# Other prices for VectorE, ScalarE and TensorE in a planner that interleaves side streams with matmuls, and a wait for free memory places in one stream

## The chip, the cores and the metric

The kernel runs on one core of a Trainium2 chip. Five engines work side by side, each through its own instructions in order: TensorE (PE in the profile: matmuls, and PEld: its weight loads), VectorE (DVE), ScalarE (ACT), GpSimd (POOL) and SyncE (SP), which here starts transfers. Semaphores make an engine wait for another. The metric is the device time of one execution in microseconds (us).

## The reference

One layer with a prompt of 512 tokens and 8 samples of 16 tokens each, 640 tokens in all, in float32. Every token goes through a wide input product, whose columns feed three branches; their gated sum goes through a normed residual and a feed-forward part.

```python
z = x @ w_in
xa, ya, glu, q, gates = jnp.split(z, COL_SPLITS, axis=-1)
xa_c = causal_depthwise_conv(xa_hist, conv_a_w, conv_a_b)
h, h_last = rg_lru(xa_c, h_prev, lru_w_r, lru_b_r, lru_w_i, lru_b_i, lru_lambda)
out_a = (h * jax.nn.gelu(ya)) @ proj_a
u = glu[..., :D_CONV] * jax.nn.sigmoid(glu[..., D_CONV:])
v = causal_depthwise_conv(u_hist, conv_b_w, conv_b_b)          # 31 taps, 512 channels
out_b = jax.nn.silu(layer_norm(v, ln_b_g, ln_b_b)) @ proj_b
out_c = mem_cross_attention(q, mem_k, mem_v) @ proj_c          # 4 heads, 256 memory rows
merged = g[:, :, 0] * out_a + g[:, :, 1] * out_b + g[:, :, 2] * out_c
x = layer_norm(DEEPNORM_ALPHA * x + merged @ w_out, ln1_g, ln1_b)
ffn = (jax.nn.silu(x @ w_ffn_gate) * (x @ w_ffn_up)) @ w_ffn_down
x = layer_norm(DEEPNORM_ALPHA * x + ffn, ln2_g, ln2_b)
```

## The kernel before

Data lie with features on the 128 partitions and the 640 tokens along the free side. A float32 product is made of three products of a shorter type (xh by wh, xl by wh, xh by wl, where h is the rounded part and l the rest), so each weight tile is copied (wh, on ScalarE) and its rest subtracted (wl, on VectorE, or on POOL for every second step from 12 to 35: line 305).

The program is a list of 304 steps. A step of w_in makes 128 output columns: 8 blocks of the inner size, times three products, times two halves of 320 tokens, 48 matmuls into two accumulators named pu, and then an evacuation that reads them. There are four pu accumulators, so step i+2 can start only when step i has been evacuated. Steps 8 to 11 and 16 to 19 make the glu columns, 12 to 15 the queries, 20 to 27 xa, 28 to 35 gates, 36 to 43 are proj_c's, which need the attention's output.

Beside the steps run side streams, written as generators: `b` (the convolution of 31 taps over four tiles k = 0 to 3, all on VectorE, its states and its norm ln_b), `attn` (the prompt's attention in four row tiles t, then the samples'), `lru` and `a`. Their small matmuls go to two other accumulators named pv; `room()` lets a stream go on when one is free. Each engine's program order is fixed when the program is written, by a planner: every issued instruction adds its price (`price_vector`, `price_scalar`, `price_tensor`) to a clock of its engine, and between two half steps `advance()` lets the streams issue work as long as the clocks of VectorE and ScalarE are behind that of TensorE:

```python
while max(V.time, 0 if name in vector_next else A.time) < P.time:
    c = next(gen)
```

`finish(name)` issues all that is left of a stream at once. A stream holds its temporary tiles in 52 memory places; `slots_left(n)` yields while fewer than n are free.

Four places matter. `softmax_start` reads a score accumulator with a maximum on VectorE (mx), its negative (nm), and four exponentials on ScalarE; it is called for each t of the prompt and for the samples. `conv_b_taps(k)` issues 30 pairs of VectorE instructions for tile k, of 128x(512 minus the tap) and 128x128. `conv_b_states` stands between tiles 1 and 2. ln_b begins with a sum of the four tiles on POOL (lines 853 and 855), which a matmul by the tile `ones` reads. Nearly all engine instructions are recorded on line 64, where the planner's wrapper calls the engine.

Of the kernel before, what the change touches and what calls it, by code (L numbers as in the profile page):

```python
# [39 lines left out]
def view(x, shape):  # L40

    n = 1
    for d in shape[1:]:
        n *= d
    x = x[:shape[0], :n]
    if len(shape) == 3:
        x = x.rearrange("p (a b) -> p a b", a=shape[1])
    elif len(shape) == 4:
        x = x.rearrange("p (a b c) -> p a b c", a=shape[1], b=shape[2])
    return x  # L50
# [17 lines left out]
def elements(x):  # L68
    n = 1
    for d in x.shape[1:]:  # L70
        n *= d
    return n


def price_vector(e, name, a, k):
    if name in ("tensor_reduce", "bn_stats"):
        return 70 + elements(a[1]) / 0.96
    n = elements(a[0])
    if name == "tensor_tensor_scan":
        return 70 + 2 * n / 0.96  # L80
    if name in ("tensor_scalar", "tensor_copy", "memset"):
        return 70 + n / 1.92
    return (130 if name == "scalar_tensor_tensor" else 70) + n / 0.96


TABLES = {AF.Exp: "e", AF.Tanh: "esgl", AF.Sigmoid: "s", AF.Sqrt: "q", AF.Silu: "l", AF.Gelu_apprx_tanh: "g"}
# [2 lines left out]
def price_scalar(e, name, a, k):  # L89
    if name != "activation":  # L90
        return 100
    t = 130 + elements(a[0]) / 1.2
    t += 93 * sum(1 for z in ("scale", "bias", "accum_out") if z in k and not isinstance(k[z], float))
    need = TABLES.get(a[2])
    if need is not None and (e.table is None or e.table not in need):
        e.table = need[0]
        t += 1283
    return t


def price_tensor(e, name, a, k):
    n = elements(a[0])
    if a[1].dtype == F32R:
        return n / 2.4 + 2.5
    if a[0].shape[0] == 32:
        return n / 2.4
    return max(105.0, (n if name == "transpose" else 4 * n) / 2.4)


class Slots:  # L110
# [7 lines left out]
    def get(self, shape, dtype=F32):  # L118
        if not self.free_list:
            raise RuntimeError("no slot is free")  # L120
        i = self.free_list.pop(0)
        self.low = min(self.low, len(self.free_list))
        self.count += 1
        x = self.pool.tile([128, T], dtype, name=f"s{i}_{self.count}", tag=f"s{i}", bufs=1)
        x = view(x, shape)
        self.at[id(x)] = (i, x)
        return x

    def free(self, *xs):
        for x in xs:  # L130
            i, _ = self.at.pop(id(x))
            self.free_list.append(i)
# [11 lines left out]
def trunk(ctx, tc, x_prompt, x_sample, mem_prompt, state_conv_a, state_lru, state_conv_b, cache_mem_k, cache_mem_v,  # L144
# [4 lines left out]
          new_conv_a_s, new_lru_s, new_conv_b_s):  # L149
    nc = tc.nc  # L150
    V, A, P = Engine(nc.vector, price_vector), Engine(nc.scalar, price_scalar), Engine(nc.tensor, price_tensor)
    G, S = nc.gpsimd, nc.sync

# [15 lines left out]
    def slots_left(n):  # L169
        while len(slots.free_list) < n:  # L170
            yield None
# [7 lines left out]
    def pv():  # L179
        assert side[0] < 2  # L180
        side[0] += 1
        return ps.tile([128, 2, 512], F32, name="pv", tag="v", bufs=2)

    def room(n=1):
        while side[0] + n > 2:
            yield None

    def over(n=1):
        side[0] -= n
# [16 lines left out]
    def split(hi, lo, src, eng=V):  # L206
        copy(hi, src)
        eng.tensor_tensor(lo, src, f32(hi), op=OP.subtract)
# [111 lines left out]
    def stream(name, gen):  # L320
        streams.append((name, gen))
# [521 lines left out]
    def token_row(cols):  # L843

        p = pv()
        for t in range(5):
            P.transpose(p[:, t // 4, (t % 4) * 128:(t % 4 + 1) * 128], cols[:, t:t + 1].to_broadcast([128, 128]), ident)
        return p

    def ln_b_stream():  # L850
        def total(x):
            y = get([128, T])
            G.tensor_tensor(y, x[0], x[1], op=OP.add)
            for k in range(2, KC):
                G.tensor_tensor(y, y, x[k], op=OP.add)
            return y

        y = total(vb)
        yield 1
        yield None  # L860
        yield from room()
        p = pv()
        P.matmul(p[:, 0], ones, y[:, :512], start=True, stop=True)
        P.matmul(p[:, 1, :128], ones, y[:, 512:], start=True, stop=True)
        free(y)
        yield None
        over()
        sq = []
        for k in range(KC):
            V.tensor_sub(vb[k][:, :512], vb[k][:, :512], p[:, 0])  # L870
            V.tensor_sub(vb[k][:, 512:], vb[k][:, 512:], p[:, 1, :128])
            x = get([128, T])
            A.activation(x, vb[k], AF.Square)
            sq.append(x)
            yield 1
        y = total(sq)
        free(*sq)
        yield 1
        yield None
        yield None  # L880
        yield from room()
        p = pv()

        for t in range(5):
            P.matmul(p[:, 0, t * 100:(t + 1) * 100], y[:, t * 128:(t + 1) * 128], ones[:, :100], start=True, stop=True)
        free(y)
        yield None
        over()
        ve = small.tile([128, 5], F32, name="ve5")
        V.tensor_scalar(ve, p[:, 0, :500].rearrange("p (t n) -> p t n", n=100)[:, :, 0], EPS, None, op0=OP.add)  # L890
        rs = small.tile([128, 5], F32, name="rs5")
        G.tensor_tensor(rs, ve, mhalf[:, :5], op=OP.pow)
        yield 1
        yield from room()
        p = token_row(rs)
        yield None
        over()
        for k in range(KC):
            V.tensor_mul(vb[k][:, :512], vb[k][:, :512], p[:, 0])
            V.tensor_mul(vb[k][:, 512:], vb[k][:, 512:], p[:, 1, :128])  # L900
            yield 1
        for k in range(KC):
            A.activation(vb[k], vb[k], AF.Silu, scale=pb[:, k, 32:33], bias=pb[:, k, 33:34])
        yield 1
        for k in range(KC):
            hi, lo = get([128, T], F32R), get([128, T], F32R)
            split(hi, lo, vb[k])
            free(vb[k])
            bT[k] = (hi, lo)
            yield 1  # L910
# [36 lines left out]
    def attn_prompt():  # L947
# [89 lines left out]
        for jobs in (((k_turn, 0),), ((k_split, 0), (scores, 0)), ((soft_a, 0), (scores, 1)), ((soft_b, 0), (soft_a, 1)),  # L1037
                     ((turn, 0), (soft_b, 1), (scores, 2)), ((turned_split, 0), (soft_a, 2), (turn, 1)),
                     ((turned_split, 1), (soft_b, 2), (scores, 3)), ((soft_a, 3), (values, 0), (turn, 2)),
                     ((queries, 0), (values_split, 0), (turned_split, 2), (soft_b, 3)), ((turn, 3),),  # L1040
                     ((turned_split, 3),), ((values, 1),), ((values_split, 1),)):
            for f, i in jobs:
                if f in matmuls:
                    yield from room()
                r = f(i)
                if r is not None:
                    yield from r
            yield 1
            yield None
        for i in range(2):  # L1050
            free(*kT[i])
            free(*vN[i])
# [317 lines left out]
    def a_stream():  # L1370
        for j in range(KD):
            while j not in hs or j not in gel:
                yield None
            h = hs.pop(j)
            V.tensor_mul(h, h, gel[j])
            free(gel[j])
            hi, lo = get([128, T], F32R), get([128, T], F32R)
            copy(hi, h)
            yield None
            V.tensor_sub(lo, h, f32(hi))  # L1380
            free(h)
            aT[j] = (hi, lo)
            yield 1
# [496 lines left out]
    def begin_attn():  # L1880
        stream("attn", chain(attn_prompt(), attn_sample()))
        stream("b", chain(conv_b_stream(), ln_b_stream()))

    def reach(i):
        if i == 0:
            x_stats(0)
            pump(1)
            last_x()
            pump()
            load_rows()  # L1890
        if i == first["glu"] + 4:
            finish("param")
            stream("b", chain(conv_b_stream(), ln_b_stream()))
        if i == first["q"] + 4:
            streams.insert(0, ("attn", chain(attn_prompt(), attn_sample())))
        if i == first["pairs"] - 6:
            streams.insert(len(streams) - 1, ("sums0", sums_stream(lambda: state["i"] >= first["pairs"])))
        if i == first["pc"] - 5:
            stream("lru", lru_stream())
            stream("a", a_stream())  # L1900

    n = len(steps)
    prepped = 0
    for i, s in enumerate(steps):
# [54 lines left out]
```

## Time and profile before

| | |
|---|---|
| median of three runs | 1100.27 us (1099.83 to 1100.51) |
| the profiled execution | 1099.67 us |
| its span | 1097.9 us |
| TensorE busy | 1061.7 us (97%) |
| VectorE, ScalarE, POOL busy | 802.9, 490.1, 165.3 us |

The span is the stretch of the trace from the first to the last instruction; 1.77 us of the execution's time lie around it. TensorE's share says that it bounds the kernel over its length, so time is lost where its matmuls wait for data or run at a lower granted clock. VectorE's 73% is a mean: it is full in some stretches.

### The profile page before, as it was taken

How to read it: one execution, taken by the hardware profiler on the slowest of the kernel's cores; microseconds unless marked ns; L12 is line 12 of the kernel's file. 1: busy time of each engine (PE TensorE's matmuls, PEld its weight loads, DVE VectorE, ACT ScalarE, POOL GpSimd, SP SyncE). 2: the span in 40 equal slices, each digit the busy share in tenths (PEclk: the TensorE clock that was granted, in tenths of full speed). 3: DMA queues.
4: the chain of work that ended last, by engine and by line, in shares of the span. 5: the costliest groups of instructions: out<-in, count | busy, mean ns of one | idle time of the engine just before them, and what ended most of it. 6: DMA issues, size and time to landing. Idle time of an engine off the chain costs nothing.

```text
span 1097.9 us, 17000 instructions
## 1 busy us (share of the span) xinstructions
PE 1061.7 (97%) x6827; PEld 1005.9 (92%) x6827; DVE 802.9 (73%) x1335; ACT 490.1 (45%) x863; POOL 165.3 (15%) x185
## 2 busy tenths in 40 slices
PE   8799898998999999999999999899999999999997
PEld 6699898997999999999999889899999999888886
DVE  6929898996364873779855678888887887544775
ACT  4532645446648445846523124433444444334341
POOL 3623323556200000010001120000000000100111
PEclk9999999998999999999999999999999999999999
DMA  9732123352412121212325331132222322734481
GB/s 340 253 95 78 39 67 97 118 154 65 147 52 83 59 96 59 95 45 78 115 78 172 135 134 59 39 101 92 77 78 85 108 77 78 287 115 137 162 289 45
DMA packets 80334, 123.11 MB, mean 112 GB/s; under 512 B 4075, under 2 KB 59371, under 8 KB 80256
## 3 DMA queue, kind: packets, MB, share of 16 engines
q1 hardware_dynamic: 73168, 100.36, 27.6%
q0 software_dynamic: 7088, 21.68, 6.2%
q8 instruction: 53, 0.87, 0.3%
q14 instruction: 25, 0.20, 0.1%
HBM read 112.41 MB, written 9.61 MB: 111 GB/s over the span
## 4 chain that ended last, share of the span: by engine, by line
PE 70%; DVE 11%; ACT 4%; issue 1%; DVEq 0%; ACTq 0%
PE pu L64 62%; DVE s L64 10%; PE pv L64 8%; ACT s L64 3%; ACT L64 1%; DVE wl L64 1%; ACT wh L64 0%; DVE xres L64 0%; DVE mx L64 0%; DVE wh L64 0%; DVE xl L64 0%; DVE nm L64 0%; DVEq L1955 0%; ACT wl L64 0%; DVE st L64 0%
## 5 line engine op out<-in xcount | busy, mean ns | idle before, releaser
L64 PE MATMUL pu<-xh,wh 128*128 128x320 f32 x1040 | 252.6, 315 | 8.3 <-ACT s L64 7.1
L64 PE MATMUL pu<-xh,wl 128*128 128x320 f32 x1040 | 246.9, 310 | 0.0
L64 ACT ACTIVATE wh<-wr 128x1024 fp32r<-128x1024 f32 (+1 forms) x149 | 134.9, 908 | 229.1 <-PE pu L64 123.2
L64 PE MATMUL pu<-xl,wh 128*128 128x320 f32 x888 | 219.7, 311 | 0.0
L64 PEld LDWEIGHTS pu<-xh,wh 128*128 128x128 f32 x1040 | 178.1, 190 | 13.2 <-ACT s L64 9.1
L64 PE MATMUL pu<-s,wh 128*128 128x320 f32 x1064 | 185.5, 310 | 1.9 <-DVE s L64 1.3
L64 PEld LDWEIGHTS pu<-xh,wl 128*128 128x128 f32 x1040 | 177.4, 189 | 0.1
L64 DVE TENSOR_TENSOR s<-s,s 128x640 fp32r<-128x640 f32 (+4 forms) x176 | 124.5, 723 | 65.5 <-ACT s L64 63.3
L64 PEld LDWEIGHTS pu<-s,wh 128*128 128x128 f32 x1064 | 163.4, 188 | 3.4 <-DVE s L64 2.4
L64 DVE TENSOR_TENSOR wl<-wr,wh 128x1024 fp32r<-128x1024 f32 (+1 forms) x100 | 114.1, 1141 | 66.7 <-ACT wh L64 66.7
L64 PEld LDWEIGHTS pu<-xl,wh 128*128 128x128 f32 x888 | 154.2, 189 | 0.6 <-DVE xl L64 0.6
L64 DVE TENSOR_TENSOR s<-s,pu 128x320 f32<-128x320 f32 x188 | 88.4, 484 | 85.8 <-PE pu L64 83.3
L64 PE MATMUL pu<-s,wl 128*128 128x320 f32 x808 | 147.3, 310 | 0.9 <-DVE s L64 0.9
L64 DVE SCALAR_TENSOR_TENSOR s<-s,pb,s 128x511 f32<-128x511 f32 (+14 forms) x240 | 130.1, 613 | 7.8 <-ACT s L64 7.8
L64 ACT ACTIVATE s<-s 128x640 fp32r<-128x640 f32 (+4 forms) x144 | 87.9, 629 | 101.9 <-DVE s L64 101.8
L64 PEld LDWEIGHTS pu<-s,wl 128*128 128x128 f32 x808 | 126.1, 188 | 1.1 <-issue 1.1
L64 PE MATMUL pu<-wh,s 128*128 128x512 f32 (+1 forms) x396 | 116.2, 386 | 0.3 <-ACT wh L64 0.3
L64 PEld LDWEIGHTS pu<-wh,s 128*128 128x128 f32 x396 | 73.1, 189 | 15.1 <-ACT wh L64 1.2
L64 ACT ACTIVATE s<-pu 128x320 f32<-128x320 f32 (+2 forms) x90 | 36.7, 442 | 68.1 <-PE pu L64 68.0
L64 PE MATMUL pu<-wl,s 128*128 128x512 f32 (+1 forms) x198 | 62.9, 389 | 1.6 <-POOL wl L305 0.8
L305 POOL TENSOR_TENSOR wl<-wr,wh 128x1024 fp32r<-128x1024 f32 x13 | 44.4, 3418 | 81.2 <-ACT wh L64 68.4
L64 PE MATMUL pv<-wh,s 128*128 128x512 f32 (+1 forms) x152 | 48.7, 367 | 0.4 <-DVE xres L64 0.4
(139 smaller groups left out, 1249.0 us busy)
## 6 DMA issues: line engine op xcount, KB each, us to landing
wr<-in_w_in SPq DMA_DIRECT2D x26, 1024.0 KB, 5.1
wr<-in_w_ffn_down SPq DMA_DIRECT2D x19, 1024.0 KB, 5.1
wr<-in_w_ffn_gate SPq DMA_DIRECT2D x11, 1024.0 KB, 5.3
wr<-in_w_ffn_up SPq DMA_DIRECT2D x11, 1024.0 KB, 5.3
s<-in_cache_mem_k POOLq DMA_DIRECT2D x16, 256.0 KB, 7.0
s<-in_cache_mem_v POOLq DMA_DIRECT2D x16, 256.0 KB, 7.2
wr<-in_proj_a SPq DMA_DIRECT2D x4, 1024.0 KB
wr<-in_w_out SPq DMA_DIRECT2D x4, 1024.0 KB, 5.7
```

Source lines behind the costliest of these rows:

```text
L64: return f(*a, **k)
L305: self.eng.tensor_tensor(l, x, f32(h), op=OP.subtract)
```

## The change

The three price functions get other numbers while a flag `sparse` is set, which is from the first step until the prompt's attention has been issued; after that, VectorE's prices are as before but for scalar_tensor_tensor (150 for 130) and the divisor, ScalarE's have a divisor of 1.18, and TensorE's are as before. ln_b's loop of squares yields until three memory places are free.

```diff
+sparse = [True]
+
 def price_vector(e, name, a, k):
+    base = 140 if sparse[0] else 70
     if name in ("tensor_reduce", "bn_stats"):
-        return 70 + elements(a[1]) / 0.96
+        return base + elements(a[1]) / 0.96
     n = elements(a[0])
     if name == "tensor_tensor_scan":
-        return 70 + 2 * n / 0.96
+        return base + 2 * n / 0.955
     if name in ("tensor_scalar", "tensor_copy", "memset"):
         return 70 + n / 1.92
-    return (130 if name == "scalar_tensor_tensor" else 70) + n / 0.96
+    return (base + 80 if name == "scalar_tensor_tensor" else base) + n / 0.955
...
-    t = 130 + elements(a[0]) / 1.2
+    t = (180 if sparse[0] else 130) + elements(a[0]) / 1.18
...
     if a[1].dtype == F32R:
-        return n / 2.4 + 2.5
+        return n / 2.4 + (13.3 if sparse[0] else 2.5)
...
             V.tensor_sub(vb[k][:, 512:], vb[k][:, 512:], p[:, 1, :128])
+            yield from slots_left(3)
             x = get([128, T])
             A.activation(x, vb[k], AF.Square)
...
             yield 1
             yield None
+        sparse[0] = False
         for i in range(2):
             free(*kT[i])
...
+    sparse[0] = True
     n = len(steps)
```

The order of TensorE's, VectorE's, ScalarE's and POOL's instructions differs from step 13 to some 40% of the program; before and behind that it is the same, and SyncE's transfers keep their order. The three places below are those that the prediction speaks of. Numbers at the end of a name tell buffers apart.

VectorE, at the end of the convolution's taps, before: tile k = 3 is s1_131, its last taps have 483 and 482 columns, and the samples' softmax (mx, nm) stands behind the last one.

```order
L64 SCALAR_TENSOR_TENSOR s1_131_2299<-s49_80_1412,pb_86,s1_131_2299 128x483
L64 SCALAR_TENSOR_TENSOR s1_131_2299<-s9_58_690,pb_86,s1_131_2299 128x128
L64 SCALAR_TENSOR_TENSOR s1_131_2299<-s49_80_1412,pb_86,s1_131_2299 128x482
L64 SCALAR_TENSOR_TENSOR s1_131_2299<-s9_58_690,pb_86,s1_131_2299 128x128
L64 TENSOR_REDUCE mx_2747<-pv_2223 128x4
L64 TENSOR_SCALAR nm_2749<-mx_2747 128x4
L64 TENSOR_TENSOR wl_2719<-wr_2432,wh_2718 128x1024
```

The same place now, where tile k = 3 is s7_141:

```order
L64 SCALAR_TENSOR_TENSOR s7_141_2465<-s49_80_1404,pb_86,s7_141_2465 128x487
L64 SCALAR_TENSOR_TENSOR s7_141_2465<-s9_58_690,pb_86,s7_141_2465 128x128
L64 TENSOR_TENSOR s42_165_2781<-s30_163_2778,s31_164_2780 128x512
L64 TENSOR_TENSOR s51_168_2787<-s43_166_2784,s50_167_2786 128x512
L64 TENSOR_REDUCE mx_2802<-pv_2274 128x4
L64 TENSOR_SCALAR nm_2804<-mx_2802 128x4
L64 SCALAR_TENSOR_TENSOR s7_141_2465<-s49_80_1404,pb_86,s7_141_2465 128x486
L64 SCALAR_TENSOR_TENSOR s7_141_2465<-s9_58_690,pb_86,s7_141_2465 128x128
```

The maximum has moved ahead of the last five tap pairs (486 to 482 columns), and two subtractions for the samples' values have moved ahead of it.

ScalarE, around the samples' four exponentials, before: they stand between two table loads and ahead of the evacuation (pu_2613, pu_2614) of step 29.

```order
L64 ACTIVATE wh_2718<-wr_2432 128x1024
L64 ACT_TABLE_LOAD
L64 ACTIVATE s48_163_2752,sm_2751<-pv_2223,nm_2749 128x256 x2
L64 ACTIVATE s30_164_2753,sm_2751<-pv_2223,nm_2749 128x256 x2
L64 ACT_TABLE_LOAD
L64 ACTIVATE s31_169_2769<-pu_2613,pa_85 128x320
L64 ACTIVATE s31_169_2769<-pu_2614,pa_85 128x320
```

ScalarE there now, where pu_2660 and pu_2661 are step 30's accumulators and pu_2764 is of step 31:

```order
L64 ACT_TABLE_LOAD
L64 ACTIVATE s32_169_2807,sm_2806<-pv_2274,nm_2804 128x256 x2
L64 ACTIVATE s33_170_2808,sm_2806<-pv_2274,nm_2804 128x256 x2
L64 ACT_TABLE_LOAD
L64 ACTIVATE s25_171_2815<-pu_2660,pa_85 128x320
L64 ACTIVATE s25_171_2815<-pu_2661,pa_85 128x320
L64 ACTIVATE wh_2849<-wr_2598 128x1024
L64 ACTIVATE s14_176_2890<-pu_2764,pa_85 128x320
```

The exponentials have moved one step later and now stand ahead of the evacuation of step 30 instead of step 29.

TensorE, at the ones matmul of ln_b, before: it stands in the middle of step 30, 24 matmuls behind the place at which the last tap is issued.

```order
L64 MATMUL pu_2721<-xh_83,wl_2500 128x320
L64 MATMUL pu_2722<-xh_83,wl_2500 128x320
L64 MATMUL pv_2766<-s15_162_2714,ones_81 128x512
L64 MATMUL pv_2766<-s15_162_2714,ones_81 128x128
L64 MATMUL pu_2721<-xh_83,wh_2499 128x320
```

TensorE there now, at the end of step 33; the eight transposes ahead of it are those of the samples' softmax:

```order
L64 MATMUL pu_2930<-xh_83,wl_2762 128x320
L64 MATMUL pv_3008<-ident_74,s32_169_2807 128x128 x4
L64 MATMUL pv_3008<-ident_74,s33_170_2808 128x128 x4
L64 MATMUL pv_3017<-s15_179_2959,ones_81 128x512
L64 MATMUL pv_3017<-s15_179_2959,ones_81 128x128
L64 MATMUL pu_3032<-xh_83,wh_2849 128x320
```

The ones matmul has moved some three and a half steps later, to 72 matmuls of steps behind the last tap.

## Rows read from the trace of the kernel before

**Rows 1.** The page: busy time, share of the span, instructions.

```profile
PE 1061.7 (97%) x6827; PEld 1005.9 (92%) x6827; DVE 802.9 (73%) x1335; ACT 490.1 (45%) x863; POOL 165.3 (15%) x185
```

**Rows 2.** TensorE's waits over the span: total us, times, longest us.

```profile
PE pv L64 <- POOL s L855: 5.0, 1, 5.0
```

**Rows 3.** By stretch: length, busy PE, PEld, DVE, ACT, POOL (instructions), granted clock, DMA.

```profile
107.00:147.00 40.00, 36.13 (x238) 35.07 (x239) 35.65 (x70) 20.45 (x45) 12.04 (x24) 0.96 0.18 59
147.00:187.00 40.00, 37.80 (x269) 37.00 (x268) 34.34 (x72) 24.73 (x73) 12.75 (x17) 1.00 0.15 44
187.00:244.00 57.00, 56.43 (x435) 53.72 (x439) 57.00 (x104) 25.32 (x60) 29.98 (x22) 1.00 0.53 160
244.00:266.00 22.00, 17.00 (x107) 15.32 (x97) 14.89 (x31) 11.35 (x24) 9.44 (x12) 0.84 0.26 75
345.00:435.00 90.00, 88.12 (x590) 86.41 (x589) 52.34 (x90) 47.58 (x73) 0.00 (x0) 1.00 0.20 65
550.00:575.00 25.00, 25.00 (x172) 25.00 (x171) 14.18 (x20) 6.98 (x8) 0.00 (x0) 1.00 0.27 86
```

**Rows 4.** TensorE's waits, 104 to 108 and 110 to 120, then timeline (start, us).

```profile
PE pu L64 <- DVE s L64: 1.0, 1, 1.0
...
PE pv L64 <- DVE s L64: 1.0, 2, 0.7
...
136.82 0.74 PE L64 MATMUL pu<-xh,wh 128*128 128x320 f32 x2 [2.30 <-ACT s L64]
...
168.90 0.88 PE L64 MATMUL pv<-ident,s 128*128 128x128 f32 x6 [1.15 <-ACT s L64]
...
187.57 1.10 PE L64 MATMUL pv<-s,s 128*128 128x256 f32 x7 [1.62 <-DVE s L64]
...
253.17 2.50 PE L64 MATMUL pv<-s,ones 128*128 128x512 f32 x4 [5.00 <-POOL s L855]
```

**Rows 5.** Busy time and granted clock in two stretches behind waits.

```profile
138.00:141.40 3.40, 3.40 (x15) 3.40 (x14) 3.40 (x6) 1.75 (x5) 3.28 (x1) 0.51 0.00 0
...
250.60:257.40 6.80, 4.23 (x12) 3.20 (x13) 4.56 (x9) 4.16 (x10) 5.82 (x7) 0.50 0.42 118
```

**Rows 6.** VectorE's timeline, 165 to 264: start us, us, what, count, idle before.

```profile
178.60 8.58 DVE L64 SCALAR_TENSOR_TENSOR s<-s,pb,s 128x511 f32<-128x511 f32 x12 [3.74 <-ACT s L64]
...
188.44 7.39 DVE L64 SCALAR_TENSOR_TENSOR s<-s,pb,s 128x505 f32<-128x505 f32 x16
195.75 1.41 DVE L64 TENSOR_TENSOR s<-pv,s 128x256 fp32r<-128x256 f32 x4
...
198.89 1.22 DVE L64 TENSOR_TENSOR wl<-wr,wh 128x1024 fp32r<-128x1024 f32 x1
...
251.36 1.22 DVE L64 TENSOR_REDUCE mx<-pv 128x4 f32<-128x1024 f32 x1
```

**Rows 7.** POOL's timeline, 140 to 262.

```profile
234.35 5.50 POOL L305 TENSOR_TENSOR wl<-wr,wh 128x1024 fp32r<-128x1024 f32 x1 [8.67 <-ACT wh L64]
...
251.58 1.53 POOL L855 TENSOR_TENSOR s<-s,s 128x640 f32<-128x640 f32 x1 [8.12 <-DVE s L64]
```

**Rows 8.** VectorE's groups by form, 178.6 to 252.6: busy us, mean ns.

```profile
L64 DVE SCALAR_TENSOR_TENSOR s<-s,pb,s 128x508 f32<-128x508 f32 x2 | 4.4, 2217 | 0.0
...
L64 DVE SCALAR_TENSOR_TENSOR s<-s,pb,s 128x503 f32<-128x503 f32 x2 | 1.5, 726 | 0.0
```

**Rows 9.** ScalarE's timeline, 240 to 264.

```profile
253.21 1.28 ACT L64 ACT_TABLE_LOAD   x1 [8.90 <-DVE nm L64]
...
256.45 1.28 ACT L64 ACT_TABLE_LOAD   x1
257.75 0.95 ACT L64 ACTIVATE s<-pu,pa 128x320 f32<-128x320 f32 x2
```

**Rows 10.** ScalarE's and VectorE's groups by form, 290 to 310.

```profile
L64 ACT ACTIVATE s<-pv 128x128 fp32r<-128x128 f32 x4 | 0.8, 275 | 0.0
...
L64 DVE TENSOR_TENSOR s<-pv,s 128x128 fp32r<-128x128 f32 x4 | 0.9, 284 | 9.6 <-ACT s L64 9.6
```

## Prediction

> **What bounds the kernel now.** I read the busy line first. TensorE is busy 97% of the span [rows 1], so only time in which its matmuls wait, or run below full clock, can be won. An undisturbed stretch is the yardstick: 172 matmuls in 25.00 us [rows 3], 145.3 ns each, at a granted clock of 1.00. The table of stretches then shows where TensorE falls short: 6.1 us between 107 and 187, 0.6 in the 57 us to 244, 5.0 between 244 and 266 at a mean clock of 0.84, and 1.9 in the 90 us from 345 [rows 3]. The diff can reach no matmul outside 90 to 470 us. The waits name who is late [rows 2, 4]: VectorE 1.0 us near 106, VectorE again 1.0 us in all at the first scores, ScalarE 2.30 at 136.82 (its evacuation stands behind the exponentials), ScalarE 1.15 at 168.90, VectorE 1.62 at 187.57, and 5.00 us ahead of the ones matmul at 253.17. [...]
>
> The 5.00 has this cause: the ones matmul wants POOL's sum of the four convolved tiles, the last add runs at 251.58 [rows 7], and it waited for the last convolution tap, which VectorE ended at 251.36, just ahead of the maximum mx [rows 6]. VectorE is busy without a gap from 178.60 on [rows 6], 57.00 us of 57.00 in one stretch [rows 3]. It was given more than it can do.
>
> **Why it was given too much.** A tap is a pair of instructions, 128x(512 minus the tap) and 128x128. Undisturbed, 8 pairs took 7.39 us, 0.92 each [rows 6]. The price before for a middle pair (503 columns) is 130+503/0.96+130+128/0.96 = 917 ns, so the price is right for an undisturbed pair. But from 178.60 to 251.36, 72.8 us, VectorE did 60 pairs, 8 subtractions at 0.35 (1.40 for 4, [rows 6]) and 3 weight splits at 1.2 [rows 6]: 66.4 us for 60 pairs, 1.11 each. The extra 0.19 comes where POOL reads memory: a tap of 508 columns took 2217 ns beside 726 for one of 503 [rows 8], and POOL's own subtraction took 5.50 us there [rows 7]. The price after is 220+503/0.955+220+128/0.955 = 1101 ns: the mean with POOL's disturbance in it. After the switch of `sparse` it is 961.
>
> For TensorE, the price before of 320 columns is 135.8 ns and that after 146.6; the rows say 145.3. [...]
>
> A check of this reading: 60 pairs underpriced by 0.19 make 11.4 us, and the 460 matmuls that are issued beside them, underpriced by 9.5 ns, give back 4.4, so VectorE should be 7.0 late at its last tap. The tap stands where TensorE begins a step some 24 matmuls (3.5 us) ahead of the stop at 248.17 (253.17 less 5.00), 244.6; VectorE ended it at 251.36, 6.7 late.
>
> **The change, part by part.** No instruction is added to TensorE, and the matmuls are the same; what moves is how much of the side streams stands ahead of each matmul. The places are counted in TensorE's calls in the issue order.
> - *Near 106:* 3 tap pairs fewer (2.8 us of VectorE) stand ahead of the evacuation: gain 1.0 (0 to 1.0).
> - *First scores:* they move 24 matmuls, 3.5 us, behind their split: gain 1.0 (0.7 to 1.0).
> - *At 134:* the exponentials again stand ahead of an evacuation, one step later; one table load fewer, but the maximum follows later too: 0 (between +4.0, the wait and its clock, and -1.5, an estimate from the 1.28 of a table load [rows 9]).
> - *At 168:* 7 tap pairs fewer, 6.4 us, stand ahead of the maximum of the fourth tile: gain 1.1 (0 to 1.1).
> - *At 187:* 6 pairs stood ahead of the split that `values(1)` wants, and none do now: gain 1.6 (0 to 1.6).
> Together 4.7.
> - *Ones matmul:* it stands 72 matmuls (10.5 us) behind the last tap instead of 24. Gain 5.0 + 2.1 = 7.1.
> - *Sample softmax (new wait).* Before, it stood at the ones matmul and its ScalarE part ran inside that wait. Now it stands 48 calls later, with 5 tap pairs behind it, and on ScalarE its two table loads and four exponentials stand ahead of the evacuation of step 30, whose accumulators step 32 writes. When is VectorE at the maximum? Its third tile of taps starts some 72 calls (10.1 us) later in TensorE's order, less 3.1 gained by there: 178.6+10.1-3.1 = 185.6. To the maximum it has 72.8 us less 5 pairs (4.6) and 4 subtractions (1.4), plus a weight split (1.2) and two 512-wide subtractions (1.2 together, an estimate a little under two of the 503-column taps): 69.2, or 66.6 if POOL's two adds come later than the maximum (1.3 for each, an estimate below the 1.49 that its subtraction added to a tap). So mx runs at 252.2 to 254.8. From the start of mx to the first of the two evacuations before was 251.36 to some 258.2, half of the 0.95 pair past 257.75 [rows 9]: 6.8. So step 32 may start at 259.0 to 261.6. TensorE is there at 248.17 plus 72 calls (at most 10.4) less 4.7 = 253.9. New wait 5.1 to 7.7, I take 6.4, the middle. Queued behind those exponentials are both evacuations and the next weight copies. The clock: both waits above were followed by half clock at 1.7 and 2.1, so I add 1.9 (0 to 2.1). Loss 8.3.
> - *Step 36.* The attention streams end later, so `finish("attn")` now forces their tail: a copy of 128x512, four transposes, copies of 0.275 and subtractions of 0.284 each [rows 10], then proj_c's matmuls, with nothing between. Before, other matmuls covered this. One copy, one subtraction and what of the big copy is not over when the transposes want it: 0.75 to 1.5, I take 1.1; 2.4 if a table load (1.28, [rows 9]) gets between.
> - *`slots_left(3)`* issues nothing. It holds the norm's squares back while fewer than 3 places are free, which they now are around step 35 (none left); ln_b ends after step 42 instead of before step 37, and is wanted at step 46, ten matmul steps of cover: 0. Without that cover `finish("b")` would stop TensorE for its silu and two products.
> - *345 to 470:* the lru and a streams find the same work at other places. Lost before 1.9 [rows 3]; 0, by up to 1.5 either way.
> Sum: 4.7 + 7.1 - 8.3 - 1.1 = 2.4 gained. The profiled execution took 1099.67, of which 1097.9 is span; 1099.67 - 2.4 = 1097.3. The median, 1100.27, is 0.6 above that execution, and I forecast it for the profiled execution's like; the 0.6 is inside the range.
>
> **The rivals.** A measurement here tells about 0.2%, 2.2 us, from no change.
> - *A, the full gain.* If VectorE reaches mx by 247, TensorE never waits at step 32. For it: the price now equals the mean with disturbance. Against: most of the last two tiles' taps come after the switch, at 961 against 1.11 us, so VectorE runs late again: 43 pairs by 0.15 less 360 matmuls by 9.5 ns, 3 us. 1099.67 - 4.7 - 7.1 + 1.1 = 1089.0; with the stop at 134 gone as well 1085.0. Chance 0.14.
> - *B, no change.* The lateness goes with POOL, not with the price: the same four POOL subtractions lie in the taps. If it falls ahead of mx and puts that at 256 to 257, the new wait is 8.9 to 9.9 and its clock 1.9, and all is given back: 1099.8 to 1100.8. Chance 0.20. [...]
> - *C, slower.* What is put off lands on the evacuations of steps 33 to 46: attention a step later, ln_b six steps later, on top of lru and a. Each evacuation that stands behind one more wide ScalarE instruction costs up to 1.3 (a table load). It decides when more than 4 of them (2.4 + 2.2 = 4.6 us) stop TensorE; five stops (6.4) and step 36 at 2.4 give 1105. Against it: ScalarE is busy only 47.58 us of the 90 from 345, where the last of these streams stand [rows 3]. Chance 0.13.
>
> **How the numbers follow.** The sum has 0.53. Its own range is 1094.5 to 1100: the new wait between its bounds is 1.3 either way, and the smaller terms at theirs about 1.5. The bound of faster is 1098.1, 0.8 above the forecast, so of the 0.53 I give 0.38 to faster, 0.13 to same and 0.02 to slower. A adds 0.14 to faster; B 0.17 to same and 0.03 to slower; C 0.12 to slower and 0.01 to same. That makes 0.52, 0.31 and 0.17. The low end cuts off half of A, the high end most of C: 1091 to 1102.
>
> **What would show it.** Right: no wait by POOL's sum at the ones matmul; a wait of step 32 for ScalarE of 5 to 8 us, followed by half clock; no wait at 187; a stop of about 1 us at step 36. Wrong: no such wait (then A), mx later than 256 (B), or new ScalarE waits between 270 and 350 (C).

## The result

The changed kernel is slower by a quarter of a per cent: 1103.26 us (median of 10 runs, 1101.43 to 1103.68) against 1100.36 before (10 runs, 1099.83 to 1101.31), a ratio of 1.0024 with a 95% interval of 1.0014 to 1.0034. The forecast was 1097.3, with 1091 to 1102 for the range. The span of the profiled execution went from 1097.9 to 1101.7 us, 3.8 longer.

Three of the stretches of [rows 3] in the profile after, in the same columns, with the stretch behind the new wait as the last:

```profile
107.00:147.00 40.00, 37.58 (x255) 37.16 (x255) 34.90 (x66) 19.36 (x47) 11.32 (x24) 0.96 0.24 79
147.00:187.00 40.00, 40.00 (x290) 39.93 (x289) 32.52 (x76) 24.94 (x74) 11.77 (x13) 1.00 0.20 60
...
244.00:266.00 22.00, 12.66 (x83) 11.49 (x82) 11.86 (x19) 10.88 (x21) 12.88 (x12) 0.82 0.67 209
...
258.10:268.30 10.20, 5.78 (x21) 5.65 (x22) 7.81 (x17) 8.92 (x20) 1.55 (x1) 0.50 0.01 4
```

TensorE lost nothing from 147 to 187 (2.2 before), and 2.4 instead of 3.9 from 107 to 147. But it was busy 12.66 us of the 22 from 244, against 17.00 before. For the whole balance a second cut is needed, since the stretches behind the wait matter too. Before, then after:

```profile
100.00:230.00 130.00, 122.93 (x871) 119.26 (x870) 119.99 (x236) 64.89 (x169) 48.60 (x60) 0.99 0.33 99
230.00:275.00 45.00, 39.95 (x297) 36.21 (x296) 36.33 (x58) 24.84 (x45) 27.34 (x22) 0.92 0.24 72
275.00:350.00 75.00, 75.00 (x590) 73.81 (x589) 40.05 (x76) 44.59 (x66) 8.18 (x9) 1.00 0.32 101
...
475.00:515.00 40.00, 38.52 (x261) 37.57 (x261) 33.73 (x56) 22.22 (x44) 4.12 (x8) 1.00 0.14 45
```

```profile
100.00:230.00 130.00, 127.16 (x909) 124.75 (x908) 115.24 (x237) 66.00 (x170) 61.24 (x57) 0.99 0.30 92
230.00:275.00 45.00, 35.66 (x247) 33.71 (x246) 28.23 (x49) 19.84 (x37) 28.49 (x16) 0.89 0.35 106
275.00:350.00 75.00, 71.00 (x576) 67.57 (x575) 40.19 (x79) 39.86 (x62) 16.13 (x19) 1.00 0.28 85
...
475.00:515.00 40.00, 37.31 (x246) 37.01 (x244) 32.86 (x51) 22.26 (x40) 4.12 (x8) 0.96 0.18 57
```

TensorE's busy time rose by 4.2 us in the first stretch and fell by 4.3, 4.0 and 1.2 in the three others that are shown; the 125 us between them (350 to 475) gave back 1.1. So TensorE stood idle 4.2 us more, close to the 3.8 by which the span grew; its busy time over the whole span is the same within 0.3 (1061.7 and 1061.4). The half clock behind waits (0.50 in the stretch from 258.10 above) lies inside the busy time; what made up for it there was not traced. TensorE's waits in the profile after, over the span and then from 100 to 230:

```profile
PE pu L64 <- ACT s L64: 19.9, 6, 9.3
...
PE pu L64 <- ACT s L64: 2.4, 1, 2.4
PE pv L64 <- DMA s<-in_cache_mem_k: 0.4, 1, 0.4
```

The waits of [rows 4] near 106, at the first scores, at 168, at 187 and at the ones matmul are gone. The one near 134 stayed (2.4 for 2.30), a new one of 0.4 for a transfer came, and waits of step matmuls (pu) for ScalarE went from 7.6 to 19.9 in all, the longest 9.3. That longest is the first matmul of step 32:

```profile
262.52 1.05 PE L64 MATMUL pu<-xh,wh 128*128 128x320 f32 x2 [9.34 <-ACT s L64]
```

To see what was late, its cause is followed back by engine. ScalarE's evacuation of step 30 at 261.94 stands behind the samples' exponentials, which stand behind the maximum:

```profile
251.77 0.64 ACT L64 ACTIVATE s<-s 128x512 fp32r<-128x512 f32 x1 [6.03 <-DMA s<-in_lru_w_r]
...
257.40 1.28 ACT L64 ACT_TABLE_LOAD   x1 [4.04 <-DVE nm L64]
...
261.94 0.95 ACT L64 ACTIVATE s<-pu,pa 128x320 f32<-128x320 f32 x2
```

VectorE (the mean of 36 instructions in 16.48 us is 0.458, 0.92 a tap pair, as undisturbed as in [rows 6]):

```profile
183.56 3.78 DVE L64 SCALAR_TENSOR_TENSOR s<-s,pb,s 128x511 f32<-128x511 f32 x8 [0.30 <-ACT s L64]
...
188.40 3.76 DVE L64 SCALAR_TENSOR_TENSOR s<-s,pb,s 128x507 f32<-128x507 f32 x8
...
193.97 8.56 DVE L64 SCALAR_TENSOR_TENSOR s<-s,pb,s 128x503 f32<-128x503 f32 x18
...
203.59 11.78 DVE L64 SCALAR_TENSOR_TENSOR s<-s,pb,s 128x494 f32<-128x494 f32 x26
217.06 4.14 DVE L64 SCALAR_TENSOR_TENSOR s<-s,pb,s 128x511 f32<-128x511 f32 x8 [1.70 <-ACT s L64]
...
222.26 16.48 DVE L64 SCALAR_TENSOR_TENSOR s<-s,pb,s 128x507 f32<-128x507 f32 x36
238.68 1.21 DVE L64 TENSOR_TENSOR wl<-wr,wh 128x1024 fp32r<-128x1024 f32 x1
239.81 4.91 DVE L64 SCALAR_TENSOR_TENSOR s<-s,pb,s 128x489 f32<-128x489 f32 x6
252.44 3.56 DVE L64 TENSOR_TENSOR s<-s,s 128x512 fp32r<-128x512 f32 x2 [7.71 <-ACT s L64]
255.92 1.21 DVE L64 TENSOR_REDUCE mx<-pv 128x4 f32<-128x1024 f32 x1
```

POOL:

```profile
206.37 11.25 POOL L309 TENSOR_TENSOR wl<-wr,wh 128x1024 fp32r<-128x1024 f32 x1 [4.62 <-PE pv L64]
...
225.10 17.04 POOL L309 TENSOR_TENSOR wl<-wr,wh 128x1024 fp32r<-128x1024 f32 x1
...
245.06 0.75 POOL L1255 DMA_DIRECT2D s<-in_lru_w_r  x1
...
253.58 1.87 POOL L859 TENSOR_TENSOR s<-s,s 128x640 f32<-128x640 f32 x1
```

VectorE had done all taps that stand ahead of the maximum by 244.72 (239.81 + 4.91). Then it stood idle for 7.71 us, in front of the two 128x512 subtractions that stand ahead of mx in the order shown with the change. Those were taken there for the samples' values. They are the rests of the lru weights, which wait for their rounded parts on ScalarE (251.77), and these for their transfer, which POOL asked for only at 245.06. In its order POOL could not ask sooner: a weight subtraction that stands ahead of the request, of a kind that took 5.50 at most in this stretch before [rows 7], took 17.04 us, while VectorE's taps ran on beside it. The chain is POOL's subtraction, its transfer, ScalarE's copy, VectorE's two subtractions (3.56 for both, with POOL's add of 253.58 beside them), mx, exponentials, evacuation, step 32. Behind the wait the granted clock was 0.50 for 5.78 busy us (stretch 258.10 above). The 22 step matmuls that began from 262.52 on took the 6.01 us to 268.53, where at the 145.3 ns of the undisturbed stretch they take 3.20: a loss of 2.8. Half of the 5.78, 2.9, is the estimate that the expectation of e1 has.

### The profile page after: what moved, and what is told of

The parts are those of the page before. It is cut to its first block, busy times and chain, and to the rows that moved or that the text cites. A ratio compares the mean times of both kernels' runs of the same rounds, so it can differ in the third digit from the quotient of the medians.

```text
span 1101.7 us, 16996 instructions
## 1 busy us (share of the span) xinstructions
PE 1061.4 (96%) x6827; PEld 1008.3 (92%) x6827; DVE 793.2 (72%) x1335; ACT 487.3 (44%) x861; POOL 185.8 (17%) x185
## 4 chain that ended last, share of the span: by engine, by line
PE 86%; DVE 3%; ACT 3%; POOL 3%; DMA 2%; issue 2%; SPq 0%; DVEq 0%; POOLq 0%; ACTq 0%
PE pu L64 75%; PE pv L64 10%; ACT s L64 2%; DVE s L64 2%; POOL wl L309 1%; ACT L64 1%; DMA s<-in_cache_mem_k 1%; POOL s L544 1%; DMA s<-in_lru_w_r 1%; DMA s<-in_w_mem_k 1%; POOL s L545 1%; DVE xres L64 0%; DMA s<-in_x_prompt 0%; POOL s L1075 0%; ACT wh L64 0%
## 5 line engine op out<-in xcount | busy, mean ns | idle before, releaser
L64 DVE TENSOR_TENSOR s<-s,s 128x640 fp32r<-128x640 f32 (+4 forms) x176 | 126.9, 736 | 70.2 <-ACT s L64 67.8
L64 DVE SCALAR_TENSOR_TENSOR s<-s,pb,s 128x511 f32<-128x511 f32 (+14 forms) x240 | 122.8, 583 | 6.1 <-ACT s L64 6.1
L64 PEld LDWEIGHTS pu<-wh,s 128*128 128x128 f32 x396 | 73.1, 189 | 15.2 <-ACT wh L64 1.2
L309 POOL TENSOR_TENSOR wl<-wr,wh 128x1024 fp32r<-128x1024 f32 x13 | 65.9, 5070 | 97.8 <-ACT wh L64 84.8
L1783 POOL DMA_DIRECT2D xres<-x x5 | 2.6, 534 | 275.5 <-DVE wl L64 275.0
```

The source lines that it names most:

```text
L64: return f(*a, **k)
L309: self.eng.tensor_tensor(l, x, f32(h), op=OP.subtract)
L1783: G.dma_start(r[:, t], scratch["x1"][t * 128:(t + 1) * 128, :])
```

## The experiments

All runs were timed in three rounds beside the kernel before; ratios are to it, with 95% intervals. A trace shows one execution; where that one lies at the edge of a run's times, the text says so. Kernel by kernel:

| run | what | us | ratio |
|---|---|---|---|
| e1_early_load | after, lru weights asked for at step 26 | 1098.46 | 0.9984 (0.9974 to 0.9993) |
| e4_lru_later | after, lru and a start one step later | 1092.60 | 0.9934 (0.9915 to 0.9952) |
| e2_pool_splits_off | after, no weight rests on POOL from step 27 | 1096.74 | 0.9969 (0.9956 to 0.9982) |
| e5_both | e4 and e2 | 1088.09 | 0.9889 (0.9872 to 0.9905) |
| p_tensor | TensorE's price alone | 1108.76 | 1.0079 (1.0064 to 1.0094) |
| p_vector | VectorE's prices alone | 1093.33 | 0.9928 (0.9903 to 0.9953) |
| p_scalar | ScalarE's price alone | 1097.67 | 0.9980 (0.9971 to 0.9990) |
| p_no_scalar | all but ScalarE's | 1093.18 | 0.9939 (0.9924 to 0.9954) |
| e6_before_pool | before, no weight rests on POOL from step 27 | 1098.28 | 0.9981 (0.9971 to 0.9991) |
| e7_vec_pool | p_vector and e2's edit | 1081.14 | 0.9824 (0.9809 to 0.9838) |
| e8_ns_pool | p_no_scalar and e2's edit | 1085.58 | 0.9862 (0.9847 to 0.9877) |
| e11_before_later | before, lru and a one step later | 1113.45 | 1.0115 (1.0099 to 1.0130) |

The wait of ln_b for free places can't be taken out under the new prices: without it the changed order holds more tiles at a time than there are places. With the old prices and that wait the instruction order is that of before, so in that order it costs nothing. What it costs in the changed order was not measured.

**Is it the transfer? e1_early_load**

```diff
+        if i == first["pc"] - 10:
+            ri_load(0)
         if i == first["pc"] - 5:
             stream("lru", lru_stream())
...
     def ri_prep(q):
+        if (q, "r") not in ri_raw:
+            ri_load(q)
         for n, w in (("r", lru_w_r), ("i", lru_w_i)):
-            raw = get([128, 4, 128])
-            G.dma_start(raw, w[0, 4 * q:4 * q + 4].rearrange("n c d -> c n d"))
+            raw = ri_raw.pop((q, n))
```

> The changed kernel, but the first two transfers of lru weights are issued by POOL at step 26 instead of step 31; no other instruction moves on any engine. Theory T (transfer): in the changed kernel the samples' maximum is late because two subtractions ahead of it on VectorE wait 7.71 us for lru weights, which POOL asked for only at 245.06, behind a weight subtraction of 17.04 us. Then VectorE's gap of 7.7 is gone, mx runs by 248, the wait of step 32 for ScalarE shrinks from 9.34 to under 2 and its half clock goes: 1103.3 - 9.3 - 2.9 = 1091 (1089 to 1094). Rival L (late VectorE, as predicted): mx is late because of the taps themselves; the wait stays at 5 or more and the time at 1099 or more.

4.8 us came back, not 12, and neither theory's numbers were met: T wanted 1089 to 1094, L 1099 or more. VectorE, POOL, and TensorE's waits from 100 to 350:

```profile
246.68 4.45 DVE L64 TENSOR_TENSOR s<-s,s 128x512 fp32r<-128x512 f32 x2 [1.71 <-ACT s L64]
251.06 1.21 DVE L64 TENSOR_REDUCE mx<-pv 128x4 f32<-128x1024 f32 x1
...
197.69 0.75 POOL L1257 DMA_DIRECT2D s<-in_lru_w_r  x1
...
246.21 2.40 POOL L309 TENSOR_TENSOR wl<-wr,wh 128x1024 fp32r<-128x1024 f32 x1 [0.90 <-ACT wh L64]
...
PE pu L64 <- ACT s L64: 7.6, 3, 4.8
```

The gap of 7.71 is 1.71 now, and mx runs at 251.06 instead of 255.92, 4.9 earlier, by which the longest wait fell from 9.3 to 4.8. So the late transfer is shown to be half of the wait. The other half is not the taps, as rival L has it: the gap of 1.71 that is left is a wait for ScalarE, with no tap in it. The two subtractions still stood ahead of mx. ScalarE's copies for them (246.03) stand in its order behind a weight copy at 245.07 that waited 2.15 us for TensorE, and the two then took 4.45 us, beside a POOL subtraction at 246.21 (2.40); in e2 below, where POOL subtracts nothing there, the same two take 1.29.

**Take them from ahead of the maximum: e4_lru_later**

```diff
-        if i == first["pc"] - 5:
+        if i == first["pc"] - 4:
             stream("lru", lru_stream())
```

> The changed kernel, but the lru and a streams start at step 32 instead of step 31; the samples' maximum then stands ahead of the lru weights' transfers and subtractions on VectorE. Theory T: nothing ahead of mx waits for a transfer, the wait of step 32 shrinks to under 2, and 9 to 12 us come back: 1091 to 1094, less what the later start of lru costs behind step 36 (up to 2). Rival L: the wait stays at 5 or more: 1099 or more.

It came out as theory T has it. VectorE's mx, POOL's subtraction and its request for the lru weights, and the longest wait of TensorE between 225 and 350:

```profile
245.31 1.23 DVE L64 TENSOR_REDUCE mx<-pv 128x4 f32<-128x1024 f32 x1 [1.42 <-PE pv L64]
...
224.26 17.04 POOL L309 TENSOR_TENSOR wl<-wr,wh 128x1024 fp32r<-128x1024 f32 x1
...
250.22 0.77 POOL L1255 DMA_DIRECT2D s<-in_lru_w_r  x1
...
268.27 1.08 PE L64 MATMUL pv<-s,s 128*32 128x128 f32 x32 [3.28 <-ACT s L64]
```

mx runs at 245.31, and what it waited for is TensorE's scores: VectorE is early. POOL's subtraction still takes 17.04, the weights are asked for 5 us later than in the changed kernel (250.22), and step 32 does not wait. What is left is a wait of 3.28 at 268.27.

**The control: e11_before_later**

> A control: the kernel before with lru and a started at step 32 instead of 31. Before, the lru weights stood behind the samples' maximum anyway. Theory T: the start of lru costs only where its weights stand ahead of the maximum, so nothing: 1099 to 1101. Rival: a later start of lru is good in itself (less work crowding steps 31 to 36), and e4's gain has little to do with the transfer: 1094 to 1097.

The edit is that of e4, on the kernel before. Neither expectation was met: 13 us lost, where nothing or a gain was expected. POOL, ScalarE, VectorE, TensorE:

```profile
276.46 0.75 POOL L1249 DMA_DIRECT2D s<-in_lru_w_r  x1
...
283.66 0.63 ACT L64 ACTIVATE s<-s 128x512 fp32r<-128x512 f32 x1 [14.47 <-DMA s<-in_lru_w_r]
...
284.38 1.51 DVE L64 TENSOR_TENSOR s<-s,s 128x512 fp32r<-128x512 f32 x2 [24.24 <-ACT s L64]
...
291.22 1.33 PE L64 MATMUL pv<-ident,rs 128*128 128x128 f32 x5 [11.24 <-POOL rs L892]
```

It is the same mechanism in another place. POOL's queue had seven transfers of cached values (5.21 us from 269.08) and more ahead of the lru weights, which were asked for at 276.46, so ScalarE stood 14.47 us before its copy and VectorE 24.24 before its subtraction; behind it, in VectorE's order, stood the small instruction (ve) on which POOL's rs and then ln_b's transposes wait, 11.24 us of TensorE. So in the order of before a later start of lru is not good in itself. What counts is what stands behind the two subtractions in the order when their weights come late.

**POOL: e2_pool_splits_off, e6_before_pool, e5_both**

```diff
-                 eng=G if ld is loads[0] and o == 0 or 12 <= len(steps) < 36 and len(steps) % 2 else V)
+                 eng=G if ld is loads[0] and o == 0 or 12 <= len(steps) < 26 and len(steps) % 2 else V)
```

> The changed kernel, but the weight rests of steps 27, 29, 31, 33 and 35 are subtracted on VectorE instead of POOL (the planner prices them, so some stream work moves too). Theory S (starved POOL): POOL's subtractions of 11.25 and 17.04 us were held off by VectorE's unbroken taps, and POOL's queue of transfers stood behind them. Without them the lru weights are asked for some 17 us earlier, VectorE's gap ahead of mx is gone, and the price is three to four subtractions of 1.2 us more on VectorE ahead of mx: wait of step 32 at 0 to 3, 1090 to 1095. Rival L: VectorE is the late one, so 3.6 us more on it lengthen the wait from 9.3 to about 13: 1107.

In e2, VectorE's two subtractions and the first matmul of step 32:

```profile
243.64 1.29 DVE L64 TENSOR_TENSOR s<-s,s 128x512 fp32r<-128x512 f32 x2 [5.57 <-ACT s L64]
...
252.09 0.83 PE L64 MATMUL pu<-xh,wh 128*128 128x320 f32 x2 [1.56 <-ACT s L64]
```

Step 32 waits 1.56 instead of 9.34, though VectorE got more work, so VectorE was not the late one. Its gap ahead of the two subtractions did not go, though S said so: it is 5.57, since ScalarE's copies stand behind a weight copy that waits 2.14 us for TensorE, to 242.03. But the copies now come 8.8 us sooner (243.00 for 251.77), so the gap costs little: in this run 5.57 us of idle VectorE stand beside a wait of 1.56 at step 32. The median is 1096.74, above what S said (its runs go from 1093.72 to 1100.6, and the trace is of the shortest).

> The kernel before, with its old prices, but the weight rests of steps 27, 29, 31, 33 and 35 are subtracted on VectorE instead of POOL. Theory S: VectorE was late before because POOL's four subtractions cost its taps some 11 us that no price held; without them a pair takes 0.92, as the old price says, and though VectorE gets some four subtractions of 1.2 more, they are priced. The wait of 5.0 for POOL's sum falls under 1.5 and its half clock goes: 1093 to 1097. Rival P: the old prices alone make VectorE late; the wait stays at 4 or more: 1099 to 1103.

In e6 no wait for POOL's sum is left in the trace, as S has it: in that execution, taking POOL's subtractions away was enough, with the old prices. But the trace is of the shortest of ten executions (1094.84, to 1100.0), and the median of 1098.28 lies between S's range and P's: of the 7.1 that the prediction has for that wait and its clock only 1.9 show in it. Whether the wait came back in the longer executions is left open, so this experiment favours S and does not settle it.

> The changed kernel with lru and a started at step 32 (as e4_lru_later, 1092.6) and no subtractions on POOL from step 27 on (as e2_pool_splits_off). Theory S: POOL's transfers are no longer held off and its subtractions disturb no tap, so what e4 still waits for transfers and for ScalarE near 265 goes: 1088 to 1092. Rival: five more subtractions of 1.2 us on VectorE cost as much as they free: 1092 to 1095.

1088.09, inside S's range. The two edits together give 15.2 us against the changed kernel, where e4's alone gave 10.7 and e2's 6.5: nearly the sum.

**The prices one by one: p_tensor, p_vector, p_scalar, p_no_scalar**

> TensorE's price alone is changed (146.6 ns for 320 columns while sparse), VectorE's and ScalarE's prices are those of before; slots_left(3) is in. If the lateness of VectorE is the sum of underpriced taps less underpriced matmuls (7 us before), taking away the second makes it some 11: the wait for VectorE around the ones matmul or the samples' softmax grows from 5.0 to 9 or more, 1103 to 1107, and the waits at 106, 115, 168 and 187 stay or grow. Rival: the waits are set by where POOL disturbs VectorE, not by the prices' balance: 1099 to 1101.

1108.76. The longest wait between 100 and 350 is that for POOL's sum at the ones matmul:

```profile
PE pv L64 <- POOL s L859: 10.9, 1, 10.9
```

10.9 for the 5.0 before, as the balance of underpriced taps and underpriced matmuls has it (9 or more). The time is 1.8 above the range of 1103 to 1107.

> VectorE's prices alone are changed; TensorE's and ScalarE's are those of before, and slots_left(3) is in. In this order the samples' maximum stands ahead of the subtractions for the lru weights. Theory P (prices): dearer taps take the lateness off VectorE, so the waits near 106, 115, 168, 187 and at the ones matmul go, and with no transfer ahead of the maximum no wait of 5 or more comes in their place: 1089 to 1095. Rival: VectorE's lateness goes with POOL's disturbance, not with its price: a wait of 5 or more stays, 1099 to 1102.

1093.33, inside P's range, so theory P stands by the time. Its trace is not read here, as the profiled execution took 1086.15 and the other four 1092.75 to 1094.21.

> ScalarE's price alone is changed. 38 of 4477 rows of TensorE stand elsewhere, all of them ahead of the samples' softmax. Theory P: ScalarE bounds no stretch, so nothing: 1099.5 to 1101.5, with the 5.0 at the ones matmul in place. Rival: ScalarE's price decides which evacuation the exponentials stand ahead of, and the wait near 134 changes: 1097 to 1099 or 1102 to 1104.

1097.67, 2.4 faster than before. The time lies in the rival's range, but not for its reason: the wait near 134 is still 2.5, and the 5.0 at the ones matmul is in place, as P has it. The wait of 1.15 at 168 is gone. The trace is of the longest of ten executions (1099.34), so it may not show all that the others gained.

> The changed kernel with ScalarE's price of before. The samples' softmax then stands some 80 TensorE calls earlier and the lru weights are asked for after it. Theory T: without a transfer ahead of the maximum the moved prices give what the prediction's gains say, 4.7 and 7.1, less what VectorE's lateness of some 3 us costs at the softmax (0 to 5): 1089 to 1095. Rival L: the softmax is late by the taps alone, wait of 5 or more with half clock behind it: 1098 or more.

1093.18, as T has it. With ScalarE's price of before the samples' softmax stands ahead of the lru weights, so ScalarE's new price, good in itself by 2.4, costs 10 in company: with the other two it is what puts the transfer ahead of the maximum. The three single effects, each against the median of the kernel before on its own chip (1100.27, 1100.05 and 1100.05), are +8.5, -6.7 and -2.4, in sum -0.6; together they gave +2.9. Prices do not add, since each moves the places at which the others act.

**The best: e7_vec_pool and e8_ns_pool**

> VectorE's prices alone (as p_vector, 1093.3), and no subtractions on POOL from step 27 on. Theory S: the wait of some 3.5 near 241 and the waits behind it shrink, as VectorE's taps run undisturbed and POOL's transfers are asked for in time: 1085 to 1090. Rival: VectorE, now dearly priced and with five subtractions more, puts its streams off so far that attention and ln_b stop TensorE at steps 36 to 46: 1092 or more.

> The changed prices without ScalarE's (as p_no_scalar, 1093.2), and no subtractions on POOL from step 27 on. Theory S: its waits for transfers of cached keys near 212 (1.2 in two) and the 4.5 near 270 shrink: 1086 to 1090. Rival: the 4.5 near 270 is attention's forced tail, which POOL has no part in; it stays, and the five subtractions cost what they free: 1092 to 1094.

Both are below what S said. e7 takes 1081.14, 1.8% under the kernel before. Its only wait between 100 and 350, and its stretches:

```profile
PE pu L64 <- DVE s L64: 0.6, 1, 0.6
```

```profile
100.00:230.00 130.00, 130.00 (x958) 127.59 (x957) 110.46 (x232) 68.78 (x175) 47.36 (x66) 1.00 0.38 114
230.00:275.00 45.00, 45.00 (x411) 42.32 (x411) 37.87 (x70) 22.71 (x46) 17.67 (x13) 1.00 0.37 115
275.00:350.00 75.00, 74.36 (x507) 73.58 (x506) 49.04 (x83) 46.66 (x64) 8.27 (x6) 1.00 0.21 64
```

TensorE is busy for all 175 us from 100 to 275 and for 74.36 of the next 75, at a granted clock of 1.00, where the changed kernel lost 12.2 and 4.0 (127.16 of 130, 35.66 of 45, 71.00 of 75). So here nearly the whole loss of these stretches is gone, that of the kernel before with it.

## Why the prediction was wrong

- **Near 106, first scores, 168, 187** (4.7 forecast): right. The four waits are gone. From 100 to 230 TensorE's busy time rose by 4.2; a wait of 0.4 for a transfer of cached keys is new.
- **At 134** (0): right, 2.4 for 2.30.
- **The ones matmul** (7.1): right; no wait for POOL's sum is left. Of the 7.1, 5.0 is that wait. The 2.1 for the clock behind it, the 1.9 of the next point and the 1.7 within the 4.0 at 134 are the author's estimates, the busy time of [rows 5] halved, and no run shows them as such. What the traces show is this. The four ones matmuls took 2.50 us at a granted clock of 0.50 (253.17 before) and 1.25 at 1.00 (280.26 after); pairs of step matmuls began every 0.53 us at 0.50 (263.90 to 267.64 after) and every 0.29 at 1.00 (268.53 to 269.71). Against those times at 1.00, 1.9 us were lost behind 136.82 and 2.2 behind 253.17 before, and 2.8 behind 262.52 after.
- **Sample softmax (new wait)** (8.3 lost): here the prediction failed. It put mx at 252.2 to 254.8 and the wait at 6.4; mx ran at 255.92 and the wait was 9.34, its clock cost 2.8 instead of 1.9, 12.1 in all. Both ends of the working were right: TensorE arrived at 253.18 (253.9 forecast), and step 32 began 6.6 after mx (6.8). The step that fails is "To the maximum it has 72.8 us less 5 pairs ... plus a weight split (1.2) and two 512-wide subtractions (1.2 together", and it fails twice. First, the 72.8 carried the old disturbance of the taps over, 11 us. After the change the 55 pairs ahead of the maximum took 53.4 us (the seven rows of taps above), only 2.8 more than 0.92 each, and they ended at 244.72 where the working has 251.0 to 253.6. Second, the two subtractions were counted as work, 1.2, without asking what they read: they waited 7.71 us for ScalarE's copies of weights whose transfer POOL had issued late, and took 3.56. The two errors had opposite signs; it is luck that the forecast wait looks near. e4 shows that without the pair ahead of it mx runs at 245.31, and that step 32 then waits for nothing; e1 shows 4.5 of the wait to be the late transfer's.
- **Step 36** (1.1) and **345 to 470** (0): step 36's own stop is 0.6, so that term was too large; from 350 to 475 TensorE gained 1.1. What the sum lacks are stops between and behind. From 275 to 350, TensorE lost nothing before and 4.0 now:

```profile
PE pv L64 <- DVE s L64: 1.4, 1, 1.4
PE pu L64 <- DVE s L64: 1.3, 2, 1.0
PE pv L64 <- ACT s L64: 1.0, 1, 1.0
PE pu L64 <- ACT s L64: 0.3, 1, 0.3
```

The last row and part of the second are step 36's forced tail (0.34 and 0.27 in the timeline); the others are single stops of the lru and attention products. They are not the queue of wide evacuations that C described. Which part of the change makes them was not separated; they go when lru starts later and POOL has no weight rests (0.3 in e5), and in e7. From 475 to 515 another 1.2 was lost, on a wait of 2.7 for ScalarE that is 0.5 before, and the mean granted clock there is 0.96 for 1.00 (the rows above). The prediction says "The diff can reach no matmul outside 90 to 470 us"; this wait lies outside. The wait is in e1, e2, e5, p_vector and p_tensor too, not in e4, p_no_scalar, e7 and e8; its cause is left open.
- **Rival A** had the mechanism right (VectorE is not late at the softmax once its price holds the disturbance), but took no account of the transfer. **Rival B** has a wait of 8.9 to 9.9, and 9.34 was measured, but by luck: it has mx late because POOL's subtractions slow the taps, and the taps ended early. That the lateness goes with POOL is true in another way: its subtraction held up the transfer. **Rival C** had the sign, and 4.0 us were lost in the stretch it names, but by other stops.
- **The check of the reading** (taps underpriced, matmuls underpriced, 7.0 late) is borne out by p_tensor: with the matmuls no longer underpriced, nothing is given back, VectorE is 11.4 late by the working instead of 7.0, and the wait grew from 5.0 to 10.9 (a wait is not the lateness: before they were 5.0 and 6.7).

## What to carry to other kernels

Where an order is about to change, follow every instruction that newly stands ahead of a critical one back to what it reads: here two subtractions of 1.3 us held the chain for 11, since their operands came through a transfer from a late queue. A price that holds a measured mean also holds what disturbed the measurement (here 0.19 us a tap pair, of which the changed order kept 0.05 ahead of the maximum), and the disturbance may fall elsewhere, into idle time too, once the order is new. Change the prices of a planner one engine at a time, and look at the waits of each: here VectorE's alone gains 7 us, ScalarE's gains 2, TensorE's loses 8, and all three together lose 3.

## What was not expected of the hardware

POOL's 128x1024 subtraction takes 2.40 us in e1 (246.21). The long ones, begun beside a row of taps on VectorE, did not end until that row had been broken, by an instruction of another kind or by idle time. After the change, the one begun at 206.37 ended at 217.62: VectorE's row had run to 215.37 (203.59 + 11.78), and 1.70 of idle time followed. The one begun at 225.10 ended at 242.14: the row ran on to the weight split at 238.68, and some 30 tap instructions of 0.458 went by in between. Before it is the same on a smaller scale: begun at 234.35 [rows 7], the split at 236.39, ended at 239.85. Behind either split the next tap takes 2.85 us, where undisturbed ones take 0.73 [rows 8]. Before, then after:

```profile
236.39 1.21 DVE L64 TENSOR_TENSOR wl<-wr,wh 128x1024 fp32r<-128x1024 f32 x1
...
L64 DVE SCALAR_TENSOR_TENSOR s<-s,pb,s 128x491 f32<-128x491 f32 x1 | 2.9, 2854 | 0.0
```

```profile
L64 DVE SCALAR_TENSOR_TENSOR s<-s,pb,s 128x489 f32<-128x489 f32 x1 | 2.8, 2848 | 0.0
```

Behind the idle time the first tap took 1.11 us, with POOL's subtraction still running for the first 0.56 of it. So the two kernels show the same pattern: the subtraction ends after a break in the row, and the tap behind a split takes 2.85. They differ in how far off the break is: 2.0 us from the start of POOL's instruction before, 13.6 after. The eleven weight subtractions of POOL that took more than 3.3 us in the two traces, before and after, end 2.2 to 2.3 us after the row's last tap, or after the split that broke it; why, no run here shows. Not every one begun in a row is long: one begun at 182.11 before, in a row that ran on to 187.11, took 2.42, and the tap of 508 columns beside it 3.70 (the 2217 ns of [rows 8] is the mean of that tap and an undisturbed one). The transfers that stand behind a long subtraction in POOL's order were issued after it: after the change, those of cached values from 242.08 and the one of the lru weights at 245.06.

The executions of one kernel can also differ by more than 5 us (1094.84 to 1100.0 in e6, 1093.72 to 1100.6 in e2), where those of the kernel before in the same rounds differ by 2.0 and 2.2 (1099.42 to 1101.45, 1099.07 to 1101.25). In e2 the mean granted clock goes along (0.994 at the shortest, 0.986 at the longest); in e6 it does so only in part (0.997 and 0.990, but 0.992 at 1095.18 and 0.994 at 1099.82). Which wait varies was not traced.
